# Operands of a latent attention made in the input projection, two or four heads per product, and kept in DRAM; of the split weights only the low parts stored

## The chip, the cores and the metric

The kernel runs on one core of one Trainium2 chip. Its time is the device time of one execution in microseconds (us). Three executions of the kernel before gave 2456.94, 2460.11 and 2461.5 us, so the median is 2460.11 us. A profile was taken of one further execution.

## What is computed

One decoder layer over 2048 positions of width 1024, in float32. The mixer joins four heads of a chunkwise mLSTM with eight heads of attention whose queries, keys and values come from small latents; a gated residual and a feed-forward layer of width 4096 follow.

```python
proj = rmsnorm(x, norm_pre_mix) @ w_in            # 1024 -> 1960 columns
qk_ml, v_ml, o_ml, gates = ...                    # mLSTM: conv + silu, chunkwise scan
c_q, c_kv, k_r = ...                              # latents: 256, 128 and 32 columns
q  = (rmsnorm(c_q, q_norm) @ w_uq).reshape(B, S, 8, 64 + 32)     # last 32: rotary
kv = (rmsnorm(c_kv, kv_norm) @ w_ukv).reshape(B, S, 8, 64 + 64)  # key part, value part
k  = concatenate([kv[..., :64], broadcast(apply_rope(k_r))])
h_mla = causal_softmax_attention(q, k, kv[..., 64:])
x = x + rmsnorm(concatenate([h_ml, h_mla]) @ w_out, norm_post_mix)
x = x + rmsnorm(relu(rmsnorm(x, norm_pre_mlp) @ w_up)**2 @ w_down, norm_post_mlp)
```

## The kernel before

**Number format.** TensorE multiplies in a reduced float32 format, so an operand is held as two tiles, a high part (a cast by ScalarE) and a low part (the value less the high part). A product is three matmuls, high by high, high by low and low by high. The helper `mm3` (L213 to L216) issues them, so most matmuls of the profile have the lines 214, 215 and 216, and the tile names tell them apart.

**Who sets the order.** Every piece of work is an operation of the planner `Plan` (L111): an engine, a cost, a key and what it waits for. At each step the planner takes the operation that can start first, and among those the one with the lowest key. It writes the instructions in that order, and each engine runs its own list in order. Most transfers are issued by SyncE (SP), in order too, so a store that waits for its data holds up the loads behind it.

**Input projection.** Four blocks of 512 positions. For each block, 16 units of weights of 128x1024 pass through. A unit (`unit`, L451) is eight `mm3`, 24 matmuls of 512 columns, into one of two PSUM banks (`mm`). VectorE or ScalarE empties the bank while the next unit fills the other. `values` (L890) makes the mLSTM values in the same way (tile `mv`). Weights come through `wsplit` (L400). In blocks 0 and 1 a unit is loaded raw, its high part cast by ScalarE (L416), its low part subtracted by VectorE or GpSimd (L421). In block 1 both parts are also stored in DRAM (`wparts`), and in blocks 2 and 3 both are loaded from there (`wload`, L383). `latents_in` (L561) makes the latents, and stores their two parts in DRAM (`cds`). Around these run the mLSTM chunks (`chunk`, L936; tiles `S`, `num`, `kv`, `ht`), four per block, whose state goes from chunk to chunk.

**Attention.** 320 steps: 8 heads, 4 blocks of queries and 4, 8, 12 or 16 blocks of 128 keys. A step is three matmuls of scores (tile `S`, L1515), two exponentials on ScalarE, one subtraction for the low part of the weights (`pl`, L1529, VectorE or GpSimd) and two or three matmuls with the values (`o`, L1542 to L1545). Before a head's steps its operands are made, on the same engines and between the steps of the head before:

- `prep_k` (L1419): three matmuls of 512 columns per head and block, with 64 columns of weights (tile `kk`), then a cast by ScalarE and a subtraction by VectorE.
- `prep_q` (L1382): six matmuls per head and block (tile `qq`). VectorE multiplies by a table of cosines and sines (`trig`), SP moves 32 rows to other partitions (`tr`), GpSimd adds, ScalarE casts and GpSimd subtracts (`Ql`, L1408).
- `vpair` (L1328): the values of four heads for two blocks of keys, six matmuls of 256 columns (tile `v`).
- `maxima` (L1443): for each head and block 4 to 16 matmuls (tile `m`, L1457) whose row maxima VectorE takes (L1462, L1464), which ScalarE then puts into a row of the queries. Their results pass through two banks (`m`).

The latents come back from DRAM through GpSimd's queue (`latents`, L1308; tile `c`).

**Between the two.** Memory changes hands in three switches (L1185 to L1223): `switch1` when the latents and weights are split, `switch2` after the last unit, `switch3` after the last chunk. Only then can scores, values and the odd heads' operands be placed.

## Time and profile before

| | |
|---|---|
| median of three executions | 2460.11 us |
| the profiled execution, its own time | 2458.44 us |
| its span in the trace | 2456.7 us |
| TensorE busy | 2396.5 us, 11059 matmuls |
| VectorE, ScalarE, GpSimd busy | 1773.2, 1330.1, 827.6 us |
| mean granted TensorE clock | 0.992 |
| moved by DMA | 404.36 MB |

The span runs from the first to the last recorded instruction. The input projection takes its first 453 us, the attention the next 530 or so, the output projection and the feed-forward layer the rest. "Busy" is the time in which at least one instruction of the engine is recorded. A matmul's recorded length is longer than its pitch, since the next begins before it ends: what a matmul costs is read from the distance between starts. A group's row gives line, engine, operation, tiles, shapes and count, then the busy time in us and the mean length of one in ns, then the engine's idle time ahead of the group and what ended it.

### The profile page before, as it was taken

Reading aid. Unit: us, or ns where it says so; the run is one execution under the profiler, and the core shown is the slowest. Engines: PE = TensorE matmul, PEld = TensorE weight load, DVE = VectorE, ACT = ScalarE, POOL = GpSimd, SP = SyncE. Lnnn points to the kernel's source line nnn. Section 1 sums busy time; section 2 is a strip of 40 time slices with the busy share of each in tenths; the row PEclk is TensorE's granted clock in tenths of the full one; section 3 lists DMA queues with packets and bytes.
Section 4 is the critical chain, followed back from the end, with each engine's and each line's share of the span. In section 5 each row is a group of like instructions: output and inputs, shape, how many; then the busy total and the mean of one; then the engine's idle time right before and its main releaser. Section 6 shows DMA issues by size and latency. Waiting matters only on the chain.

```text
span 2456.7 us, 33958 instructions
## 1 busy us (share of the span) xinstructions
PE 2396.5 (98%) x11059; PEld 1934.8 (79%) x11059; DVE 1773.2 (72%) x3171; ACT 1330.1 (54%) x2628; POOL 827.6 (34%) x728
## 2 busy tenths in 40 slices
PE   8999999899999999999999999999999999999996
PEld 6778788677777777678888888888888888888885
DVE  6876646578878887655876587776676687786888
ACT  5645222367777777544666656765665343433454
POOL 3432212468898888432100000000000232332334
PEclk9999999899999999999999999999999999999999
DMA  5688847500000000566776788756664535445369
GB/s 209 213 315 296 280 173 251 143 14 17 16 17 11 17 15 13 164 213 225 259 225 206 232 286 246 219 153 193 176 206 136 170 125 176 131 141 166 125 170 240
DMA packets 308266, 404.36 MB, mean 165 GB/s; under 512 B 32652, under 2 KB 209816, under 8 KB 307896
## 3 DMA queue, kind: packets, MB, share of 16 engines
q1 hardware_dynamic: 300760, 387.98, 49.3%
q0 software_dynamic: 7328, 14.21, 2.8%
q8 instruction: 87, 1.43, 0.2%
q14 instruction: 91, 0.75, 0.1%
HBM read 265.04 MB, written 134.96 MB: 163 GB/s over the span
## 4 chain that ended last, share of the span: by engine, by line
PE 80%; DVE 7%; DMA 5%; POOL 3%; issue 2%; ACT 2%; SPq 1%; DVEq 0%; POOLq 0%; ACTq 0%
PE mm L214 3%; PE mm L216 3%; PE mm L215 3%; PE S L214 2%; PE m L1457 2%; PE S L215 2%; PE S L216 2%; PE o L1542 2%; PE o L1545 2%; PE op L215 2%; PE op L214 2%; PE op L216 2%; POOL t L1556 2%; DMA hr<-hd 1%; PE mv L214 1%
## 5 line engine op out<-in xcount | busy, mean ns | idle before, releaser
L2436 POOL TENSOR_TENSOR y<-vd_0X,y 128x512 f32<-128x512 f32 x7 | 11.3, 1621 | 726.6 <-ACT vd_0X L2433 708.6
L1521 ACT ACTIVATE ph<-S 128x512 fp32r<-128x512 f32 (+1 forms) x320 | 170.3, 532 | 106.9 <-PE S L216 63.5
L1556 POOL TENSOR_TENSOR t<-t,ph 128x512 f32<-128x512 f32 (+1 forms) x192 | 211.0, 1099 | 24.2 <-ACT ph L1521 11.0
L2348 ACT CAST hh<-hr 128x512 fp32r<-128x512 f32 (+1 forms) x208 | 116.5, 567 | 170.7 <-DMA hr<-hd 46.3
L1529 DVE TENSOR_TENSOR pl<-S,ph 128x512 fp32r<-128x512 f32 (+3 forms) x272 | 157.3, 589 | 39.1 <-ACT S L1525 34.6
L214 PE MATMUL mm<-xh,wh 128*128 128x512 f32 x384 | 157.8, 411 | 11.5 <-ACT xh L358 6.7
L2353 DVE TENSOR_TENSOR hl<-hr,hh 128x512 fp32r<-128x512 f32 (+1 forms) x208 | 130.2, 635 | 38.6 <-ACT hh L2348 31.2
L1462 DVE TENSOR_REDUCE mp<-m 128x1 f32<-128x512 f32 x192 | 129.7, 684 | 33.0 <-PE m L1457 32.4
L216 PE MATMUL mm<-xh,wl 128*128 128x512 f32 x384 | 150.9, 393 | 0.2 <-DVE wl L421 0.2
L215 PE MATMUL mm<-xl,wh 128*128 128x512 f32 x384 | 151.1, 393 | 0.0
L1525 ACT ACTIVATE S<-S 128x512 f32<-128x512 f32 (+3 forms) x272 | 141.4, 520 | 0.0
L214 PE MATMUL S<-Qh,Kh 97*128 97x512 f32 (+1 forms) x320 | 123.1, 385 | 1.0 <-ACT p L1525 0.7
L1542 PE MATMUL o<-ph,V 128*128 128x512 f32 (+1 forms) x320 | 119.3, 373 | 0.0
L215 PE MATMUL S<-Ql,Kh 97*128 97x512 f32 (+1 forms) x320 | 119.0, 372 | 0.0
L1545 PE MATMUL o<-pl,V 128*65 128x512 f32 (+1 forms) x320 | 113.5, 364 | 5.5 <-DVE pl L1529 4.8
L216 PE MATMUL S<-Qh,Kl 97*128 97x512 f32 (+1 forms) x320 | 118.6, 371 | 0.0
L1457 PE MATMUL m<-Kh,Qh 96*128 96x512 f32 (+2 forms) x320 | 109.5, 382 | 1.1 <-DVE mp L1462 0.7
L2187 ACT ACTIVATE t<-t 128x512 f32<-128x512 f32 x96 | 60.6, 631 | 79.1 <-DVE t L2182 78.7
L214 PE MATMUL op<-wo,hh 128*128 128x512 f32 x256 | 101.2, 395 | 0.5 <-DVE x L1857 0.5
L215 PE MATMUL op<-wo,hh 128*128 128x512 f32 x256 | 100.0, 391 | 0.1
L216 PE MATMUL op<-wo,hl 128*128 128x512 f32 x256 | 100.0, 391 | 0.0
L214 PEld LDWEIGHTS mm<-xh,wh 128*128 128x128 f32 x384 | 72.7, 189 | 29.3 <-ACT xh L358 7.4
(6435 smaller groups left out, 7626.8 us busy)
## 6 DMA issues: line engine op xcount, KB each, us to landing
hr<-hd SPq DMA_DIRECT2D x100, 448.0 KB
hd<-t SPq DMA_DIRECT2D x128, 256.0 KB
hd<-ts SPq DMA_DIRECT2D x96, 256.0 KB
wh<-wparts SPq DMA_DIRECT2D x32, 512.0 KB
wl<-wparts SPq DMA_DIRECT2D x32, 512.0 KB
wr<-in_wu_dram SPq DMA_DIRECT2D x31, 512.0 KB
xt<-in_x_dram SPq DMA_DIRECT2D x28, 512.0 KB
xf<-xd SPq DMA_DIRECT2D x40, 256.0 KB
```

The costliest lines, as they stand in the source:

```text
L214: pe.matmul(o, ah, bh, start=start, stop=False)
L215: pe.matmul(o, ah, bl, start=False, stop=False)
L216: pe.matmul(o, al, bh, start=False, stop=stop)
L1457: pe.matmul(ps[:, :n], Qh[s][0:96, q0 : q0 + P], Kh[s][0:96, kb * TB : kb * TB + n], start=True, stop=True)
L1462: vec.tensor_reduce(mp["t"][:, j, kb : kb + 1], ps, axis=AX.X, op=ALU.max)
L1521: act.activation(t["h"][:, :w], t["S"][:, :w], AF.Exp)
L1525: act.activation(t["p"][:, :w], t["S"][:, :w], AF.Exp)
L1529: (pool if by_pool else vec).tensor_tensor(t["l"][:, :w], t["p"][:, :w], f32(t["h"][:, :w]), ALU.subtract)
L1542: pe.matmul(o0, v[:, 0:128], t["h"][:, :w], start=start, stop=stop)
L1545: pe.matmul(o1, v[:, 64:129], t["l"][:, :w], start=start, stop=stop)
L1556: pool.tensor_tensor(to, to, hv, ALU.add)
L2353: vec.tensor_tensor(t["l", m][:, :w], t["r", m][:, :w], f32(t["h", m][:, :w]), ALU.subtract)
```

## The change

The attention's operands are made during the input projection, block by block, right after the block's latents.

- Three weight units are added: 16 (keys and values), 17 (queries without their rotary part), 18 (rotary part). `operands` makes per block four key products of two heads each (`kp`, three matmuls), four value products of all eight heads for 128 positions each (`vp`, three), four query products of two heads (`qp`, six) and two rotary products of four heads (`rp`, six). They share the two banks of the units.
- A result is cast by ScalarE, copied by VectorE, and GpSimd subtracts the one from the other, in a staging tile (`sg`, four of them). SP then stores both parts in DRAM (`qkd`, `qrd`, `vd`). For rotary results VectorE multiplies three times and GpSimd adds first.
- In the attention `load_qk` and `load_v` load the finished operands; `prep_k`, `prep_q`, `prep_u`, `vpair`, `latents` and their tiles go. `maxima` gets the bank that they used as a third one.
- Weights: `wparts` holds the low parts alone. In blocks 1 to 3 (units 0 to 8) or 2 and 3 (the rest) a unit is loaded raw, ScalarE casts its high part each time, and the low part is loaded.
- To make room, the gates have one buffer in place of two and `hn` two in place of four. Some keys and leads of the planner are set anew, and the order of block 3 is written out.

```diff
-HN = 4
+HN = 2
...
-STB = (1,) * 16
+STB = (0,)*9+(1,)*10
+SG = 4
...
+LASTLINE = [16, "k0", "k1", 9, "k2", "k3", "v0", 10, "v1", "v2", "v3", 11, 17, "q0", "q1", 12, "q2", "q3", 18, "r0", "r1", 5, 6, 7, 8]
...
-    gate = [b1.tile([P, 4, TB], F32, tag=f"gate{i}", name=f"gate{i}") for i in range(2)]
+    gate = [b1.tile([P, 4, TB], F32, tag=f"gate{i}", name=f"gate{i}") for i in range(1)]
...
+        a = pl.op("SP", 500, load, [g], kA(b, at - WLEAD), kb=n / 2)
+        c = pl.op("Activation", n * 0.833 + 110, hi, [a], kA(b, at - SPLIT), take=("wh",), free=[("awr", g)])
+        gl = pl.op("X", 0, place_l, [g, *o_turn], kA(b, at - LLEAD), take=("wl",))
+        l = pl.op("SP", 500, load_l, [gl, *o_parts[u]], kA(b, at - LLEAD), kb=n / 2)
...
+        def product(u, passes, parts, nm, n, evac, key, head, o_in):
...
+            def mm(k):
+                if k == 0:
+                    q["p"] = psm.tile([P, TB], F32, tag="mm", name=f"{nm}{b}_{n}")
+                mm3(q["p"], *parts(k), k == 0, k == passes - 1)
...
+        def two_parts(nm, n, q, last, first, key, store, kb):
+            def hi():
+                act.copy(q["s"][:, 0], q["p"])
...
+            def raw():
+                vec.tensor_copy(f32(q["s"][:, 1]), q["p"])
...
+            def lo():
+                pool.tensor_tensor(q["s"][:, 1], f32(q["s"][:, 1]), f32(q["s"][:, 0]), ALU.subtract)
...
+            g = pl.op("X", 0, place, [last], key, take=("sg",))
+            h = pl.op("Activation", 570, hi, [g, last], key, free=[("mm", first)])
...
+            d = pl.op("DVE", 690, raw, [g, last], key, free=[("mm", first)])
+            d = pl.op("Pool", 1300, lo, [h, d], key)
...
+            return [pl.op("SP", 500, lambda i=i: store(i), [d], key, free=[("sg", h)], kb=kb) for i in range(2)]
...
+                x = pl.op("DVE", 690, a1_, [last, o_tb], key + PQ, take=("sg",), free=[("mm", first), ("cbc", o_tb)])
...
+                y = pl.op("DVE", 690, a2_, [last, o_tb], key + PQ, take=("cth",), free=[("mm", first), ("cbc", o_tb)])
+                z = pl.op("DVE", 690, a3_, [y], key + PQ, free=[("mm", first), ("cbc", o_tb)])
...
+    def load_qk(h, b, key):
+        s, bs, r = h % 2, slice(b * TB, (b + 1) * TB), slice(h % 4 * 16, h % 4 * 16 + 16)
...
         def load():
...
+            dma(f32(QK[s][0:64, :, bs]), qkd[h, :, :, bs])
+            for i in range(2):
+                dma(f32(QK[s][64 + 16 * i : 80 + 16 * i, 0:2, bs]), qrd[h // 4, 64 * i + r.start : 64 * i + r.stop, :, bs])
...
+                dma(f32(V[:, t + d, :, 0:128]), vd[t + d, :, 4 * g : 4 * g + 4])
...
-            pool.dma_start(both[b][:, i : i + n].rearrange("p i x t -> p (i x) t"), cds[b][2 * i : 2 * i + 2 * n].rearrange("x p t -> p x t"))
...
-        a = pl.op("PE", 6 * 228, mm, [o_u[h][0], o_cl[0, b], o_cl[1, b], o_s3 if s else o_s2] + war, key, take=(qring("q", h),), free=[("uq", o_u[h][1])])
...
-        a = pl.op("PE", 3 * 228, mm, [o_uk, o_cl[2, b], o_s3 if s else o_s2] + war, key, take=(qring("k", h),))
...
+        def ring(i):
+            return "q" if (h, qb) in EARLY or i % 3 == 2 else "m"
```

How the change moves instructions is shown at two places. The first is VectorE's list in block 2, from the emptying of unit 9's bank (`mm2_9`). Before:

```order
L932 TENSOR_TENSOR gate0_117<-mm2_9_2838,rsbc2_2092 128x512
L875 SCALAR_TENSOR_TENSOR kT0_115<-cth2_3_2919,cy2_3_2877 128x512
L929 TENSOR_SCALAR gate0_117<-gate0_117,col_61 128x512
L932 TENSOR_TENSOR gate0_117<-mm2_10_2890,rsbc2_2092 128x512
L929 TENSOR_SCALAR gate0_117<-gate0_117,col_61 128x512
```

And in the change, where `kp2_2`, `kp2_3` and `vp2_0` are products, `ks` and `vs` their staging tiles, and the rows of `sm22_2` and `kw2_3` belong to the mLSTM:

```order
L1131 TENSOR_TENSOR gate0_116<-mm2_9_3471,rsbc2_2446 128x512
L1224 TENSOR_TENSOR sm22_2_3535<-sm22_2_3535 128x4
L1225 TENSOR_SCALAR sm22_2_3535<-sm22_2_3535 128x4
L1226 SCALAR_TENSOR_TENSOR sm22_2_3535<-sm22_2_3535 128x4
L1197 SCALAR_TENSOR_TENSOR kw2_3_3578<-kt2_3_3563,tm2_3121 128x256
L1128 TENSOR_SCALAR gate0_116<-gate0_116,col_61 128x512
L730 COPY ks2_2_3568<-kp2_2_3556 128x512
L730 COPY ks3_2_3582<-kp2_3_3573 128x512
L781 COPY vs0_2_3597<-vp2_0_3589 128x8x64
L382 SCALAR_TENSOR_TENSOR xl3_0_3620<-xr3_0_3522,col_61,xh3_0_3609 128x512
L382 SCALAR_TENSOR_TENSOR xl3_1_3626<-xr3_0_3522,col_61,xh3_1_3618 128x512
L1131 TENSOR_TENSOR gate0_116<-mm2_10_3593,rsbc2_2446 128x512
```

Between the emptyings of two units' banks three further banks are now to be emptied, and the first of them stands behind the gate's second step (L1128), which waits for ScalarE. The second place is TensorE's list from the last chunk's products on (`num3_3`: numerators of chunk 3 of block 3; `ht3_3`: its turned result). Before, queries and keys of head 0 (`qq0_0`, `kk0_1`) follow:

```order
L988 MATMUL num3_3_4286<-C1_111,qs3_3_4201 128x258
L1005 MATMUL kv3_3_0_4299<-vext_112,kw3_3_4278 128x258
L214 MATMUL qq0_0_4306<-c_0_3995,uqh0_4023 128x512
L215 MATMUL qq0_0_4306<-c_0_3995,uqh0_4023 128x512
L216 MATMUL qq0_0_4306<-c_0_3995,uql0_4028 128x512
...
L1005 MATMUL kv3_3_1_4322<-vext_112,kw3_3_4278 128x258
L1044 MATMUL ht3_3_4339<-cst_60,hn3_3_4335 128x128 x4
L214 MATMUL kk0_1_4344<-c_1_4250,ukh_3993 64x512
...
L214 MATMUL qq0_1_4353<-c_1_4250,uqh0_4023 128x512
```

In the change the maxima of head 0 follow (`m0_1_0_0` is head 0, block 1 of queries; `QK0` holds the loaded operands):

```order
L1187 MATMUL num3_3_5011<-C1_110,qs3_3_4935 128x258
L1204 MATMUL kv3_3_1_5031<-vext_111,kw3_3_4993 128x258
L1527 MATMUL m0_0_0_0_5057<-QK0_4983 128x128
L1527 MATMUL m0_0_1_0_5059<-QK0_4983 128x256
L1527 MATMUL m0_0_2_0_5061<-QK0_4983 128x384
L1243 MATMUL ht3_3_5064<-cst_60,hn3_3_5053 128x128 x4
L1527 MATMUL m0_0_3_0_5070<-QK0_4983 128x512
L1527 MATMUL m0_1_0_0_5075<-QK0_4983 128x512
L1527 MATMUL m0_1_1_0_5080<-QK0_4983 128x512
L1527 MATMUL m0_1_0_1_5085<-QK0_4983 128x128
```

Queries, keys and values have left the opening of the attention; what stands there until the first scores is the maxima, each of which VectorE has to reduce.

More of the change, by code (lines that the diff above doesn't have):

```diff
@@ L594, in sums_ @@
                     pe.matmul(t["p"][:, i * 4 + c : i * 4 + c + 1], q["s"][:, c * P : (c + 1) * P], ones[:, 0:1], start=True, stop=True)
[L596 removed]
+            take = () if i else ("sg", "sg")
+            if i == 0 and b:
+                t["o"] = list(o_staged[b - 1])
             if b == 0:
@@ L890, in values @@
     def values(b):
-        ws = [W[b, 5 + i] for i in range(4)]
+        ws = [WT[b, 5 + i] for i in range(4)]
         def one(c):
@@ L1141, in half @@
             prev.append(o)
-            o_rope.append(pl.op("SP", 1000, store, [o], key, free=[("cth", h)], kb=256))
+            o = pl.op("SP", 1000, store, [o], key, free=[("cth", h)], kb=256)
+            o_rope.extend((o, pl.op("SP", 3000, spread, [o], key, kb=1024)))
         prev = []
@@ L1257, in trunk @@
         o_const[s] = pl.op("Pool" if s == "v" else "SP", 490 if s == "v" else 1500, fill, [o_s3 if s else o_s2], key=-99 if s == 0 else -50, kb=0 if s == "v" else 24)
-    def load_w(nm, src):
-        raw = a2.tile([P, 512], F32, tag="craw", name=f"{nm}r", bufs=2)
-        dma(raw, src)
-        wts[nm] = [raw, *wts[nm]]
-    def weights(nm, src, key, after):
-        a = pl.op("SP", 500, lambda: load_w(nm, src), [after], key=key, take=("craw",), kb=256)
-        b = pl.op("Activation", 615, lambda: act.copy(wts[nm][1], wts[nm][0]), [a], key)
-        return pl.op("DVE", 680, lambda: vec.tensor_tensor(wts[nm][2], wts[nm][0], f32(wts[nm][1]), ALU.subtract), [b], key, free=[("craw", a)])
-    o_uk = weights("uk", ukw, -90, o_s1)
-    o_uv = weights("uv", uvw, -60, o_s2)
     blocks, first, start_of = [], {}, {}
```

446 lines of the change are left out of this document (231 added, 215 removed).

## The prediction

> **What bounds the kernel now.** I read the page first, then busy time by stretches, then the waits and the chain where the stretches showed gaps, and last the groups for durations.
>
> ```profile
> span 2456.7 us, 33958 instructions
> PE 2396.5 (98%) x11059; PEld 1934.8 (79%) x11059; DVE 1773.2 (72%) x3171; ACT 1330.1 (54%) x2628; POOL 827.6 (34%) x728
> ```
>
> TensorE (PE) is recorded busy 98% of the span, so 60 us are all the idle time there is. Recorded busy time proves little by itself where matmuls overlap, so I checked the pitch. These are the first and the last of 37 consecutive starts in the input projection:
>
> ```profile
> 179.62 0.39 PE L214 MATMUL mm<-xh,wh 128*128 128x512 f32 x1
> ...
> 187.78 0.39 PE L214 MATMUL mm<-xh,wh 128*128 128x512 f32 x1
> ```
>
> 36 pitches take 8.16 us, 0.227 us each; the recorded 0.39 us contains the pipeline's delay. The stretches show where PE has gaps. The columns are the stretch and its length, then busy time and count of PE, weight loads, VectorE (DVE), ScalarE (ACT) and GpSimd (POOL), then granted clock, DMA share and GB/s:
>
> ```profile
> 120.00:180.00 60.00, 57.43 (x275) 46.34 (x274) 44.13 (x89) 25.22 (x37) 21.25 (x16) 1.00 0.88 323
> 180.00:240.00 60.00, 59.65 (x285) 49.57 (x284) 40.00 (x85) 31.42 (x80) 18.28 (x20) 1.00 0.81 285
> 240.00:300.00 60.00, 59.59 (x286) 48.02 (x285) 40.46 (x90) 19.02 (x38) 14.27 (x18) 1.00 0.88 304
> 360.00:420.00 60.00, 59.82 (x278) 48.15 (x278) 37.29 (x82) 14.75 (x30) 13.74 (x17) 1.00 0.74 256
> 454.00:464.00 10.00, 6.71 (x40) 5.27 (x39) 6.70 (x19) 2.88 (x11) 6.24 (x9) 1.00 0.81 192
> 464.00:484.00 20.00, 15.62 (x63) 10.39 (x61) 11.06 (x29) 7.90 (x18) 9.52 (x15) 0.74 0.89 229
> 484.00:504.00 20.00, 18.22 (x83) 14.64 (x84) 14.53 (x32) 9.26 (x20) 9.52 (x9) 0.83 0.07 18
> 504.00:531.00 27.00, 25.36 (x114) 18.79 (x113) 21.63 (x46) 15.29 (x32) 14.10 (x13) 0.87 0.05 11
> 700.00:900.00 200.00, 199.57 (x1046) 155.41 (x1045) 163.65 (x363) 150.62 (x315) 170.38 (x148) 1.00 0.07 15
> ```
>
> Two things stand there. The input projection and the running attention are bound by PE, at full clock, with the other engines at most 85% busy. So a matmul taken out of the attention shortens it, and one put into the projection lengthens that. The opening of the attention, 454 to 531 us, is not. Busy time times clock gives 6.7 + 11.6 + 15.1 + 22.1 = 55.5 us of work in 77 us, so 21.5 us are lost there to idleness and to the lower clock.
>
> **Matmuls removed and added.** The groups of the products that go, each for the first of the three lines of `mm3`:
>
> ```profile
> L214 PE MATMUL qq<-c,uqh 128*128 128x512 f32 x64 | 27.3, 426 | 2.1 <-DMA c<-cd 2.0
> L214 PE MATMUL kk<-c,ukh 128*64 128x512 f32 x32 | 13.2, 413 | 0.4 <-DVE tq L1395 0.4
> L214 PE MATMUL v<-uvh,c 128*128 128x256 f32 x32 | 10.0, 313 | 0.8 <-DVE V L1344 0.6 <-DVE Kl L1434 0.2
> ```
>
> Times three that is 192 matmuls of 512 columns for queries, 96 for keys, and 96 of 256 columns for values, which I count as 48 of 512. Together 336. Added per block are 4x3 for keys, 4x3 for values, 4x6 for queries and 2x6 for rotary parts, 60, in four blocks 240. The key product used 64 columns of weights and has the same recorded length as the query product with 128, so two heads in one cost what one did; that halves the keys, and with the swapped rotary columns dropped the queries go from 192 to 144. Net 96 fewer, at 0.227 us: **-21.8 us**. I take it whole, because both ends of the move lie in PE-bound stretches; only some 14 us of the removal (36 of `qq` and `kk` for head 0 and 48 narrow ones of `v`) lie in the opening and are treated with it.
>
> **Waits in the input projection.** The 56 new products share two banks with the units. Before, a bank had a unit of 24 matmuls, 5.4 us, to be emptied in; a key or value product lasts 0.68 us. The waits of today and the prices:
>
> ```profile
> L214 PE MATMUL mm<-xh,wh 128*128 128x512 f32 x384 | 157.8, 411 | 11.5 <-ACT xh L358 6.7 <-DVE raw L852 4.7
> L932 DVE TENSOR_TENSOR gate<-mm,rsbc 128x512 f32<-128x512 f32 x16 | 11.0, 688 | 11.1 <-PE mm L216 11.0
> L933 ACT ACTIVATE gate<-gate 128x512 f32<-128x512 f32 x16 | 10.1, 629 | 20.3 <-DVE gate L932 20.1
> L929 DVE TENSOR_SCALAR gate<-gate,col 128x512 f32<-128x512 f32 x16 | 8.5, 530 | 4.4 <-ACT gate L933 4.1
> L1619 DVE COPY ou<-o 65x512 f32<-65x512 f32 x32 | 21.8, 682 | 10.0 <-PE o L1545 6.7 <-issue 1.2 <-POOL Ql L1408 1.1
> L1408 POOL TENSOR_TENSOR Ql<-tq,Qh 96x512 fp32r<-96x512 f32 x32 | 41.2, 1289 | 11.6 <-ACT Qh L1405 11.0 <-PE o L1568 0.5
> ```
>
> And the way from a product through a copy to the next product, in the chain:
>
> ```profile
> 469.33 0.44 PE qq L216
> 469.80 0.70 DVE tq L1395
> 470.54 0.61 PE kk L214
> ```
>
> After a recorded end DVE starts 0.03 us later, and PE 0.04 us after DVE's end. With the pipeline's delay of 0.16 (0.39 less 0.227), a bank is free 0.93 us after PE has passed its last matmul, if DVE is at hand. Follow block 2 in the order shown. PE passes unit 9 at 0, then `kp2_2` to 0.68; `kp2_3` wants unit 9's bank, 0.93: a wait of 0.25 less the mLSTM work between. `vp2_0` wants the bank of `kp2_2`, whose copy stands behind the gate's second step: 0.19 + 0.69 + 0.04 + 0.63 + 0.04 + 0.53 + 0.68 + 0.04 = 2.84, against PE's 1.6 to 2.0: a wait of about 1. Then `mm2_10` waits 0.1. The group of three values waits some 0.5 by the same count. The queries, 1.36 us each, hide a prompt copy; the second rotary product leaves three multiplications, 2.0 us, before the next block's second bank: about 1. With the pair at the start, 3 us per block, 12 in four. If DVE or ACT has another instruction of 0.7 us ahead in half of these places, 16 to 20. mLSTM work between the products hides part. I take **+13 us**, with ends of 4 and 30.
>
> The other engines have room: DVE gains 48 copies and 24 multiplications, 50 us, ACT 56 casts and 44 more casts of weights, POOL 64 instructions of 1.3 us, over a stage whose rows above show them below three quarters busy. DMA is nearer its end. By the sizes of its tiles a block of the change moves about 35 MB (raw weights 9.7, low parts 9.7, operands 7.3, x 4.2, mLSTM and tables 4), where blocks 2 and 3 moved 26. The raw weights are read in every block now. In the rows above share and rate give 323/0.88 = 367, 285/0.81 = 352, 304/0.88 = 345, 256/0.74 = 346: about 350 GB/s at a full share. 35 MB then take 100 us, and a block lasts some 125. So DMA bounds no block on average, and I add nothing, with +5 as an end for bursts.
>
> **The opening of the attention.** Now PE waits there for the last chunk and for latents that come through GpSimd's queue:
>
> ```profile
> PE ht L1044 <- DVE hn L1037: 3.3, 1, 3.3
> ```
>
> ```profile
> 457.69 0.72 POOL c L1312
> 458.41 8.32 DMA c<-cd
> 466.86 0.76 PE qq L214
> ```
>
> In the change the loads of head 0 are on SP's list ahead of the last chunks' stores, and the chain latent, product, multiplication, move, addition, cast is gone. The wait for `ht` stays, and with three narrow maxima (0.35 us) in place of the query product (1.4) as its cover it grows by 1. After it come maxima with nothing between them, and they go at VectorE's pace:
>
> ```profile
> L1462 DVE TENSOR_REDUCE mp<-m 128x1 f32<-128x512 f32 x192 | 129.7, 684 | 33.0 <-PE m L1457 32.4
> ```
>
> Seven more until the first scores, up to 0.68 us each against PE's 0.23: 3 us lost. With the 4.3 of `ht` and some 2 for the way from the last maximum over ScalarE to the first scores that is 9, and for half clock behind such gaps and waits among the later reductions I add 6 to 7. The later opening is eased: DVE loses 16 instructions of 0.68 us (4 `tq`, 4 `Kl`, 8 `V`) and 4 additions, over 11 us out of the 47 that the rows give it from 464 to 531. So the loss is 15 to 16 us in place of 21.5: **-6 us**, ends -14 and +6. The Trainium skill, "TensorE: Matmul & The Clock Gate", Part 1, says that the array falls to half clock after an idle window of about 3.4 us and needs as long a busy one to come back. The 0.74 in the row fits that; by it, as an estimate, the longer `ht` wait alone would cost 1.7 us more than I count, and the sum would be -13.1 in place of -14.8.
>
> **The rest.** From the end of the opening, near 531, the attention stays bound by PE. Its DVE, ACT and POOL work falls with PE's, so their shares stay near today's 82, 75 and 85%. The loads of operands, 30 MB over some 450 us, find DMA at a share of 0.07. Later stages are untouched.
>
> **Sum.** -21.8 + 13 - 6 = -14.8. The profiled execution took 2458.4 us (span 2456.7 and 1.7 around it), which gives 2443.6. The median of the runs lies 1.7 above it, so I forecast **2445 us**.
>
> **Rivals.**
> - *The opening gains more, or the waits stay hidden.* For it: PE had 11 us of plain idle time in 454 to 531, much of it behind the latents, and the mLSTM's matmuls lie between the products in blocks 0 to 2. Against: reductions bind the maxima. With -12 and +5: 2431.
> - *The waits eat the gain.* VectorE's list is in order, and a copy also stands behind `xl` of the next block, which needs a load. At half a microsecond per new product, 28 us and -6, nothing is left: 2460.
> - *Staging holds the banks: slower.* A copy needs one of four staging tiles, free when the product four earlier is stored. Copy 0.7, one to three subtractions in line 1.3 to 3.9, and the store. The only landing time of the trace is of a loaded moment:
>
> ```profile
> c<-cd POOLq DMA_DIRECT2D x1, 512.0 KB, 5.8
> ```
>
>   That makes 7.8 to 10.4 us, where PE reaches the same tile again after 8 to 9 us in the tightest places. If stores land 3 us later than this, three products per block wait 3 us each, 36 us in all on top of the 13: 2481. It decides from about 4 us of extra waiting per block, which cancels the 14.8. Today's stores already hold ScalarE's casts for 5.7 us, which speaks for it:
>
> ```profile
> L416 ACT CAST wh<-wr 128x1024 fp32r<-128x1024 f32 x31 | 32.4, 1044 | 28.6 <-PE mm L215 18.6 <-DMA wparts<-wl 5.7 <-PE mv L216 2.0
> ```
>
>   Against it, a tile waits for four products, most of which have a unit of 5.4 us between them. The Trainium skill, "DMA: Bandwidth & Descriptors", Anatomy of one DMA, fits a transfer by some 2.0 us and its bytes over 436 GB/s: 3.2 us for these 512 KB, where the trace has 5.8. By the page the chain would be 5.2 to 7.8 us as an estimate, PE would never wait for it, and I would give this case 0.12.
> - *The change does not do what it says.* Storing low parts alone leaves the bytes as they are; that is in the sum already.
>
> **Chances.** The forecast, 2432 to 2454: 0.50. Opening or hiding better, below: 0.18. Waits eat the gain, 2455 to 2465: 0.14. Staging and other slower cases: 0.18. A measurement of this kernel tells some 0.2%, 5 us, from no change. Faster by more: 0.68; within: 0.14; slower: 0.18. The range leaves out about a tenth at either end: the better case's own lower half below 2427, the staging case's upper half above 2470.
>
> **What would show it.** Right: PE's matmuls fall by 144; the products `kp`, `vp`, `qp`, `rp` have a pitch of 0.227; idle time before `mm` and the products grows by 10 to 15 us, released by DVE and ACT; the stretch from the last unit to the last maxima of head 0 falls from 77 to about 60 us. Staging: waits of DVE `ks` and `vs` on DMA. DMA: weights `wl` or `wh` release PE. Wrong: a total above 2455, or an opening that takes as long as now.

## The result and the profile after the change

| | before | change |
|---|---|---|
| median of 5 runs each | 2460.51 us (2456.94 to 2461.5) | 2472.6 us (2466.99 to 2473.14) |
| profiled execution: time, span | 2458.4, 2456.7 us | 2470.98, 2469.2 us |

The ratio is 1.0046, with a 95% interval of 1.0032 to 1.0061: the change is slower by half a per cent. The prediction was 0.6% faster. (Measured once more beside the last experiments, the change stood at 1.0058, 1.0043 to 1.0074.) The new page begins:

```profile
span 2469.2 us, 34097 instructions
## 1 busy us (share of the span) xinstructions
PE 2391.8 (97%) x10915; PEld 1920.1 (78%) x10915; DVE 1769.7 (72%) x3160; ACT 1359.8 (55%) x2638; POOL 811.1 (33%) x705
```

PE has 144 matmuls fewer, as counted, and almost the busy time of before: the recorded busy time of a matmul stretches where it waits or runs at half clock, so the busy share hides the loss. To find it, cut both traces at the same events. From the groups by tile: the last product of the projection's values (`mv`), the reduction that closes the maxima of a block of queries (`mx`), and the first transpose behind the attention (`xtr`). The two times in a row are the first and the last start. Before:

```profile
L216 PE MATMUL mv<-wh,xl x128: 388/389/402, 76.2 to 453.2; 128*128 128x512 f32 x128
L1908 PE MATMUL xtr<-cst,x x64: 270/273/332, 1072.1 to 1136.7; 128*128 128x128 f32 x64
530.90 0.17 DVE L1483 TENSOR_REDUCE mx<-mp 128x4 fp32r<-128x16 f32 x1
```

And in the change:

```profile
L222 PE MATMUL mv<-wh,xl x128: 388/390/629, 62.4 to 538.8; 128*128 128x512 f32 x128
L1971 PE MATMUL xtr<-cst,x x64: 270/273/330, 1085.0 to 1151.6; 128*128 128x128 f32 x64
591.17 0.16 DVE L1553 TENSOR_REDUCE mx<-mp 128x4 fp32r<-128x16 f32 x1
```

With the last `mx`, at 985.6 us before and at 995.9 us in the change, this gives:

| stretch | before | change | difference | the prediction's terms |
|---|---|---|---|---|
| input projection, to the last `mv` | 453.2 | 538.8 | +85.6 | +54.4 matmuls, +13 waits = +67.4 |
| opening, to the last maxima of head 0 | 77.7 | 52.4 | -25.3 | -13.6 matmuls, -6 = -19.6 |
| heads 1 to 7 | 454.7 | 404.7 | -50.0 | -62.7 matmuls |
| to the first `xtr` | 86.5 | 89.1 | +2.6 | 0 |
| the rest | 1384.6 | 1384.2 | -0.4 | 0 |
| sum | 2456.7 | 2469.2 | +12.5 | -14.8 |

(Matmul terms: 240 added and 336 removed, of which 60 in the opening, at 0.227 us.) Of the 27.3 us between forecast and result the projection has 18.2, the heads 1 to 7 have 12.7, the tail 2.2, and the opening gave 5.7 more than expected. A second profile of the changed kernel, told of below, differs from this one by 2 us in the projection and by 3 in the opening; smaller differences between single profiles are not read here.

**The projection.** 85.6 us less 54.4 us of new matmuls leaves 31 us. The view of PE's waits in this stretch (sum, number, longest), for the change and then for before:

```profile
...
PE kp L220 <- DVE raw L1051: 3.6, 1, 3.6
PE mm L220 <- ACT ks L727: 2.9, 4, 1.5
PE mm L221 <- DVE xl L382: 2.7, 4, 0.7
PE mv L220 <- DVE raw L1051: 2.4, 1, 2.4
PE kv L1204 <- DVE kw L1197: 2.2, 2, 1.6
PE vp L220 <- DVE gate L1131: 1.4, 1, 1.4
...
PE vp L220 <- ACT vs L778: 1.0, 3, 0.4
...
```

```profile
...
PE mm L214 <- DVE raw L852: 4.7, 4, 1.7
PE tp L764 <- DVE rrc L491: 1.5, 1, 1.5
...
```

`raw`, a bank of the mLSTM's convolution, was waited for before as well. New among the releasers are the copies and casts of operands (`ks`, `vs`) and the gates whose banks the products take. The idle times in this view leave out the pipeline's delay, so I also went over all pitches of consecutive matmuls up to the last `mv` and took from each what its kind needs undisturbed (0.2265 us for 512 columns). The excess is 66.2 us, before 37.1. Waits of units and products for an operand or gate bank are 15.7 of it, in 32 places (none before). Pitches of big matmuls without any wait hold 23.7, before 16.7. Waits for weights and inputs hold 4.8, before 1.2. The rest, 22.0 and 19.2, lies at the mLSTM's small matmuls, its waits and the banks of its convolution (`raw`). The first unit starts 1.35 us later, too.

Half clock is part of the 7.0 us by which the pitches without a wait grew. It can be seen behind the longest of these waits, in PE's timeline of the change:

```profile
457.19 0.39 PE L221 MATMUL kp<-cl,wh 128*128 128x512 f32 x1
457.42 0.40 PE L222 MATMUL kp<-ch,wl 128*128 128x512 f32 x1
461.41 0.79 PE L220 MATMUL kp<-ch,wh 128*128 128x512 f32 x1 [3.59 <-DVE raw L1051]
462.00 0.63 PE L221 MATMUL kp<-cl,wh 128*128 128x512 f32 x1
...
464.13 0.63 PE L220 MATMUL mm<-xh,wh 128*128 128x512 f32 x1
```

Ahead of the wait the pitch is 0.23 us; behind it five pitches from 462.00 to 464.13 take 0.426 each, so every such matmul costs nearly its own length again. How much of the projection ran so is told by the granted clock (the figure after the engines' counts), below 1.00 in three stretches of the change:

```profile
60.00:90.00 30.00, 27.08 (x121) 21.94 (x122) 27.96 (x47) 15.58 (x34) 11.37 (x15) 0.94 0.67 214
450.00:480.00 30.00, 24.83 (x99) 18.50 (x97) 23.36 (x31) 13.31 (x27) 13.00 (x12) 0.94 0.66 196
480.00:510.00 30.00, 29.21 (x118) 23.08 (x119) 14.16 (x23) 12.95 (x19) 12.35 (x11) 0.94 0.87 280
```

Before, it was 1.00 from 60 to 453 us. Six hundredths of 30 us are 1.8 us, so the clock cost the projection 5 us at most; the 17 pitches between big matmuls that ran at half clock hold 3.7. About as much again is the first pitch behind a wait, which is some 0.11 us longer at full clock too: 39 such pitches, six before.

**Two readers take turns.** This is the piece of the change's timeline in which block 0 makes its third and fourth key products (the second column is the duration):

```profile
110.06 0.40 PE L222 MATMUL kp<-ch,wl 128*128 128x512 f32 x1
110.50 0.69 DVE L730 COPY ks<-kp 128x512 f32<-128x512 f32 x1
...
111.11 0.40 PE L222 MATMUL kp<-ch,wl 128*128 128x512 f32 x1
...
111.22 0.58 ACT L727 CAST ks<-kp 128x512 fp32r<-128x512 f32 x1 [1.74 <-DVE ks L730]
...
111.55 0.69 DVE L730 COPY ks<-kp 128x512 f32<-128x512 f32 x1 [0.28 <-PE kp L222]
111.83 1.28 ACT L1132 ACT_TABLE_LOAD   x1
111.86 0.50 PE L220 MATMUL vp<-wh,ch 128*128 128x512 f32 x1 [0.35 <-ACT ks L727]
...
113.66 0.57 ACT L727 CAST ks<-kp 128x512 fp32r<-128x512 f32 x1
```

VectorE copies the bank and ScalarE casts it, each straight from the bank, and the cast begins 0.03 us after the copy has ended though ScalarE sat idle for 1.74 us. A bank is thus held for 0.69 + 0.03 + 0.58 = 1.30 us, not for 0.69. For the last product it is worse: between copy (111.55) and cast (113.66) ScalarE loads a table and computes a gate. So both the turns and the place in an engine's list can hold a bank; the experiments with casts take them apart.

**Heads 1 to 7.** From one head's last maxima to the next the change takes 56.3 to 56.8 us, but head 4 takes 65.0. The heads' share of the view of waits has one entry that fits, and the timelines of SP, then of VectorE, ScalarE and PE, show its cause:

```profile
PE o L1612 <- DVE ot L1685: 6.6, 1, 6.6
```

```profile
780.76 8.47 SPq L1500 DMA_DIRECT2D V<-vd  x6
...
790.71 1.14 SPq L1500 DMA_DIRECT2D V<-vd  x2
...
795.08 4.84 SPq L1500 DMA_DIRECT2D V<-vd  x4
800.64 2.30 SPq L1695 DMA_DIRECT2D hT<-ot  x1
```

```profile
805.12 0.69 DVE L1689 COPY ou<-o 65x512 f32<-65x512 f32 x1 [4.23 <-DMA sumd<-ou]
807.40 0.58 ACT L1682 COPY ot<-o 64x512 f32<-64x512 f32 x1 [7.19 <-DMA hT<-ot]
808.84 0.76 PE L1612 MATMUL o<-ph,V 128*128 128x512 f32 x1 [6.57 <-DVE ot L1685]
```

The values of heads 4 to 7 take the place of those of heads 0 to 3, so their 16 loads of 256 KB, the first four issued at 774.75 us, can start only as the last products of head 3 release them. The output rows `ot` and `ou` have one buffer each; their stores stand behind these loads, and the next rows can't be moved out of PE's banks until they have landed. The stretches around it (length, busy time and count of PE, loads, DVE, ACT and POOL, clock, DMA share, GB/s):

```profile
780.00:802.00 22.00, 21.04 (x112) 15.60 (x111) 16.32 (x37) 14.56 (x32) 15.43 (x13) 1.00 1.15 224
802.00:808.00 6.00, 0.27 (x2) 0.10 (x1) 0.69 (x1) 0.58 (x1) 0.07 (x1) 0.83 0.67 166
808.00:812.00 4.00, 3.16 (x9) 2.31 (x10) 2.54 (x5) 2.25 (x6) 2.75 (x3) 0.50 0.17 35
```

DMA is full for 22 us at 224 GB/s, PE then stands still for 6.6 us, and after that runs at half clock.

### The profile page after: what moved, and what is told of

Read it like the earlier page. It is cut to its first block, busy times and chain, and to the rows that moved or that the text cites. A ratio compares the mean times of both kernels' runs of the same rounds, so it can differ in the third digit from the quotient of the medians.

```text
span 2469.2 us, 34097 instructions
## 1 busy us (share of the span) xinstructions
PE 2391.8 (97%) x10915; PEld 1920.1 (78%) x10915; DVE 1769.7 (72%) x3160; ACT 1359.8 (55%) x2638; POOL 811.1 (33%) x705
## 3 DMA queue, kind: packets, MB, share of 16 engines
q1 hardware_dynamic: 341448, 446.98, 58.4%
## 4 chain that ended last, share of the span: by engine, by line
PE 78%; DVE 7%; DMA 6%; issue 3%; POOL 2%; ACT 2%; SPq 1%; DVEq 0%; POOLq 0%; ACTq 0%
PE S L220 2%; PE o L1612 2%; PE mm L220 2%; PE o L1615 2%; PE S L221 2%; PE S L222 2%; PE mm L222 2%; PE mm L221 2%; PE m L1527 2%; PE op L220 1%; PE op L222 1%; PE op L221 1%; DMA hr<-hd 1%; PE mv L220 1%; PE mv L221 1%
## 5 line engine op out<-in xcount | busy, mean ns | idle before, releaser
L1591 ACT ACTIVATE ph<-S 128x512 fp32r<-128x512 f32 (+1 forms) x320 | 170.2, 532 | 97.2 <-PE S L222 28.9
L1599 DVE TENSOR_TENSOR pl<-S,ph 128x512 fp32r<-128x512 f32 (+3 forms) x272 | 157.0, 590 | 30.9 <-ACT S L1595 28.9
L2416 DVE TENSOR_TENSOR hl<-hr,hh 128x512 fp32r<-128x512 f32 (+1 forms) x208 | 130.2, 635 | 36.6 <-ACT hh L2411 28.9
L220 PE MATMUL S<-QK 97*128 97x512 f32 (+1 forms) x320 | 123.7, 386 | 5.9 <-DVE pl L1599 4.7
L221 PE MATMUL S<-QK 97*128 97x512 f32 (+1 forms) x320 | 118.6, 371 | 0.0
L1527 PE MATMUL m<-QK 96*128 96x512 f32 (+3 forms) x320 | 114.9, 405 | 3.4 <-DVE mp L1532 1.8
L222 PE MATMUL S<-QK 97*128 97x512 f32 (+1 forms) x320 | 118.1, 369 | 0.0
```

The costliest lines, as they stand in the source:

```text
L220: pe.matmul(o, ah, bh, start=start, stop=False)
L221: pe.matmul(o, ah, bl, start=False, stop=False)
L222: pe.matmul(o, al, bh, start=False, stop=stop)
L1527: pe.matmul(ps[:, :n], Qh[s][0:96, q0 : q0 + P], Kh[s][0:96, kb * TB : kb * TB + n], start=True, stop=True)
L1591: act.activation(t["h"][:, :w], t["S"][:, :w], AF.Exp)
L1599: (pool if by_pool else vec).tensor_tensor(t["l"][:, :w], t["p"][:, :w], f32(t["h"][:, :w]), ALU.subtract)
```

## The experiments

The ratios are each to runs of the kernel before on the same chip, with 95% intervals; the change's own is 1.0046. One per mille is 2.5 us. "Excess" is the sum over pitches in the projection explained above (change 66.2 us, before 37.1), "bank waits" are its part of 15.7.

**No emptying of the banks.** In `two_parts`, `vevac` and `revac` the moves go; a blank tile, in the place of one of the four staging tiles, is stored.

```diff
...
-            h = pl.op("Activation", 570, hi, [g, last], key, free=[("mm", first)])
...
-            d = pl.op("DVE", 690, raw, [g, last], key, free=[("mm", first)])
-            d = pl.op("Pool", 1300, lo, [h, d], key)
...
-            return [pl.op("SP", 500, lambda i=i: store(i), [d], key, free=[("sg", h)], kb=kb) for i in range(2)]
+            pl.op("X", 0, lambda: None, [last], key, free=[("mm", first)])
+            return [pl.op("SP", 500, lambda i=i: store(i), [last, blank_op[0]], key, kb=kb) for i in range(2)]
```

> Leaves out the emptying of the operand banks: the 240 new matmuls run, but no copy, cast, subtraction or rotary multiplication follows; one blank tile is stored in the place of every operand, with the same bytes, and the attention loads and multiplies those zeros. All times on the scale on which the kernel before takes 2460.5 us and the change 2472.6. Theory evacuation (banks held by copy and cast, and the clock's fall behind these waits): the projection's excess over pure matmul time falls from 66 us to 45 or less, 2448 to 2453 us. Rival (loads and DMA make the excess): it stays above 58 and the time above 2463.

Measured 0.996 (0.9945 to 0.9975), 22 us below the change, on that scale 2450.7. The excess is 40.1 us, three more than before the change:

```profile
L222 PE MATMUL mv<-wh,xl x128: 388/389/628, 62.9 to 511.7; 128*128 128x512 f32 x128
```

The last `mv` starts at 511.7, which is 58.5 us after that of before, with 54.4 us of new matmuls. So matmuls, weights, and all the bytes that are loaded and stored cost next to nothing beyond PE's own time. (The profiled execution took 2455.68 us, 9 more than the median of the seven, and its opening 6 us more than the change's, so its total gained less than its projection.) What the forecast missed in the projection is the emptying, whole: 26 us of excess against a forecast of 13. This run doesn't tell the hold of the banks from the other work that emptying gives VectorE, ScalarE and GpSimd.

**Cast from the copy.** The cast reads SBUF, so that the bank has one reader.

```diff
-                act.copy(q["s"][:, 0], q["p"])
+                act.copy(q["s"][:, 0], f32(q["s"][:, 1]))
...
-            h = pl.op("Activation", 570, hi, [g, last], key, free=[("mm", first)])
...
             d = pl.op("DVE", 690, raw, [g, last], key, free=[("mm", first)])
+            h = pl.op("Activation", 570, hi, [g, d], key)
```

(Values in the same way.)

> The cast to the high part of keys, values and queries reads the copy in SBUF instead of the PSUM bank, so a bank is free after VectorE's copy (0.69 us) and no longer after copy and cast in turn (1.30 us). Theory bank time (the 15.7 us of waits of products and units for operand copies come from two readers taking turns): these waits fall to 6 to 9 us, the clock loses 1 to 2 us less behind them, and the time is about 2463 us. Rival, queue order (the copies are late because VectorE and ScalarE have other work ahead of them): the waits stay above 13 us and the time within 3 us of 2472.6.

Measured 1.0047 (1.0032 to 1.0063): no gain, as the rival had it, but not for its reason. Bank waits still sum to 15.6 us, in 14 places in place of 32, and half of that is one wait. The change has it in a smaller form: ScalarE's cast of the last value waits there for a store, until 128.75 us, and PE waits 0.84 us behind it (at 130.11). VectorE's, SP's and PE's timelines there:

```profile
128.52 0.69 DVE L781 COPY vs<-vp 128x512 f32<-128x512 f32 x1 [2.95 <-DMA qkd<-ks]
```

```profile
113.95 4.53 SPq L1335 DMA_DIRECT2D trep<-trigd  x6
...
119.25 4.61 SPq L757 DMA_DIRECT2D qkd<-ks  x4
```

```profile
129.36 0.77 PE L220 MATMUL mm<-xh,wh 128*128 128x512 f32 x1 [7.77 <-DVE vs L781]
```

The copy of a value waits for a staging tile, which is free when the store of a key has landed, and that store stands in SP's queue behind the six stores that spread the rotary tables in block 0. Here four of the eight key stores of this block stand behind them, in the change two (issued at 120.05 us). The remaining 13 places hold 7.7 us, which is what bank time foretold. The gain at the other places was lost at this one.

**One reader.** VectorE's copy is left out and GpSimd subtracts the cast from itself.

```diff
-                pool.tensor_tensor(q["s"][:, 1], f32(q["s"][:, 1]), f32(q["s"][:, 0]), ALU.subtract)
+                pool.tensor_tensor(q["s"][:, 1], f32(q["s"][:, 0]), f32(q["s"][:, 0]), ALU.subtract)
...
-            d = pl.op("DVE", 690, raw, [g, last], key, free=[("mm", first)])
-            d = pl.op("Pool", 1300, lo, [h, d], key)
+            d = pl.op("Pool", 1300, lo, [h], key)
```

(Values in the same way.)

> Leaves out VectorE's copy of keys, values and queries: ScalarE's cast alone reads the bank, GpSimd subtracts the cast from itself (zeros as low parts), with the same staging, stores and rotary work. Same scale; without any emptying the time was 2450. Theory bank time: a bank is held 0.6 instead of 1.3 us, bank waits fall to 5 to 8 us, 2458 to 2464. Rival staging and lists (ScalarE, GpSimd and the stores set the pace): waits above 12 us, 2468 to 2473.

Measured 1.0039 (1.0026 to 1.0052). Again a single wait takes much of the gain, at the same place; it is ScalarE's cast that lacks the tile here:

```profile
PE mm L220 <- ACT vs L777: 5.7, 1, 5.7
```

Bank waits are 14.2 us with it, 8.3 without. (The profiled execution, 2465.05 us, is one of the two fastest of five, the others took 2470 to 2471; its projection ends 5.1 us before the change's.) This run and the one before agree: halving the hold halves the waits, and staging then caps the gain. The earlier run took ScalarE's list out of the bank's way and this one VectorE's, with the same outcome, which points to the two turns rather than to the list of one engine.

**The tables' stores aside.** The six stores go through GpSimd's queue.

```diff
-                        dma(to, trigd[r0 : r0 + 16, cs].rearrange("(o j) t -> o j t", o=1).broadcast_to((n, 16, 512)))
+                        pool.dma_start(to, trigd[r0 : r0 + 16, cs].rearrange("(o j) t -> o j t", o=1).broadcast_to((n, 16, 512)))
...
-            o_rope.extend((o, pl.op("SP", 3000, spread, [o], key, kb=1024)))
+            o_rope.extend((o, pl.op("Pool", 6000, spread, [o], key, kb=1024)))
```

> The change with one edit: the six stores of the rotary tables go through GpSimd's queue, casts and output buffers as in the change. Scale as before (kernel before 2460.5, change 2472.6; early casts alone 2472, two buffers alone 2468.5, all three 2456.5). Theory staging behind the banks: with late casts PE already waits at the banks while the stores land, so the edit alone brings 0 to 3 us, 2469 to 2473. Rival (the stores in SP's queue delay weights and other loads by themselves): 2461 to 2465, and the bank waits of block 0 fall too.

Measured 1.0079 (1.0064 to 1.0093): 5 to 8 us slower than the two measurements of the change, which neither theory had. Bank waits are 21.7 us, and four of them in block 0, between 111 and 128 us, hold 7.5. GpSimd's timeline shows why:

```profile
110.30 3.73 POOL L1335 DMA_DIRECT2D trep<-trigd  x6
...
115.07 2.52 POOL L733 TENSOR_TENSOR ks<-ks 128x512 fp32r<-128x512 f32 x2
```

The issues take GpSimd for 3.7 us, the subtractions of keys stand behind them, and so the stores of keys start no earlier; VectorE's copy of a value (126.66) then waits 3.2 us for its staging tile. So the edit doesn't free the tiles sooner by itself. That explains the projection, which ends 4.4 us later than the change's; the opening and the heads 1 to 7 took 4.0 and 4.5 us more in this profile (of the slowest execution of the run), and why is open.

> Early casts and the tables through GpSimd's queue, one output buffer. Same scale. Theory: the two belong together, the shorter hold shows only once the staging wait of 8 us is gone; 2459 to 2463, with head 4 still at 65 us. Rival (the gain of all three edits came from the two buffers and chance in the order): 2468 to 2472.

With early casts as well: 1.0034 (1.0021 to 1.0048), 2468.9 us on the scale of the expectations, in the rival's range; the interval overlaps the change's. The wait of 7.8 us for staging has become one of 4.3, and head 4 still takes 63.4 us.

**Two output buffers.**

```diff
...
-... ("ot", 1, o_s3), ("ou", 1, o_s3), ...
+... ("ot", 2, o_s3), ("ou", 2, o_s3), ...
...
-            t["u"] = xrow("ou") if end else ar2.tile([P, TB], F32, tag="ou", name=f"ou{h}_{qb}", bufs=1)
+            t["u"] = xrow("ou") if end else ar2.tile([P, TB], F32, tag="ou", name=f"ou{h}_{qb}", bufs=2)
```

(`ot` in the same way.)

> The output rows of a head (ot, ou) have two buffers each instead of one. Theory burst (the 6.6 us wait of PE for ot in head 4 comes from the store of one buffer standing behind 4 MB of value loads): this wait goes, with the clock's fall behind it 7 to 9 us, about 2464.5 us, and the period of that head becomes 57 us like the others. Rival (the values themselves come too late): PE waits for V or the scores instead, the head stays at 65 us and the time at 2472.

Measured 1.003 (1.0019 to 1.004). The 6.6 us wait is gone, heads 1 to 7 take 396.2 us instead of 404.7, and head 4 takes 60.7; the six others take 335.5 together instead of 339.7, so the single buffer cost them something too. The total gained 4 us of these 8.5; the opening took 3.5 us longer in this profile, which the change's own second profile shows as scatter.

**No second load of values.**

```diff
-                    load_v(h // 4, t, W[start_of[h, qb]] - VLEAD - LDK)
+                    if h:
+                        o_v[1, t] = o_v[0, t]
+                    else:
+                        load_v(0, t, W[start_of[h, qb]] - VLEAD - LDK)
```

> Leaves out the second load of values: heads 4 to 7 use the values of heads 0 to 3 that lie in SBUF. Same scale. Theory burst: PE's 6.6 us wait for ot goes, head 4 takes 57 us like the others, 2463 to 2465. Rival (one output buffer is too few whatever the DMA does): a wait of 3 us or more for ot stays in head 4, and the time is within 3 us of 2472.6.

Measured 1.0032 (1.002 to 1.0043). Head 4 takes 56.3 us, heads 1 to 7 take 396.0, and the wait for `ot` falls from 7.5 us in the whole attention to 2.8. It is the burst: with one buffer and without the loads the wait of 6.6 us does not exist.

**Two banks for the maxima.**

```diff
-            return "q" if (h, qb) in EARLY or i % 3 == 2 else "m"
+            return "q" if (h, qb) in EARLY else "m"
```

> The maxima use two banks, as before the change, the third stays empty. Theory (the third bank eases every run of maxima in which VectorE is the slower one): the opening of the attention, 52.4 us from the last unit to the last maxima of head 0, grows by 3 to 6 us, and PE's idle time before maxima in the other heads by 2 to 6; 2478 to 2484 us in all. Rival (VectorE's pace binds the maxima whatever the number of banks): within 3 us of 2472.6.

Measured 1.0082 (1.0067 to 1.0097), 6 to 9 us slower than the two measurements of the change. The opening takes 55.6 us, no more than in the change's second profile, so nothing is seen of the theory there. Heads 1 to 7 take 406.8 instead of 404.7, and this sum hides two things: head 4 takes 61.1 us instead of 65.0, and the six others 345.7 together instead of 339.7, each of them longer (57.4 to 58.3, where the change's two profiles have 56.3 to 56.8). So the third bank is worth about 1 us in each such head; PE's idle time before maxima, 1.2 us against 1.3 in these heads, is not what makes it, so the theory's mechanism is not shown, and the cause is open.

**Pairs between units.**

```diff
-MIXED = [16, "k0", "k1", 9, "k2", "k3", "v0", 10, "v1", "v2", "v3", 11, 17, "q0", "q1", 12, "q2", "q3", 18, "r0", "r1"]
+MIXED = [16, "k0", "k1", 9, "k2", "k3", 10, "v0", "v1", 11, "v2", "v3", 12, 17, "q0", "q1", "q2", "q3", 18, "r0", "r1"]
```

(`LASTLINE` in the same way.)

> Keys and values stand in pairs between units (two keys, unit 9, two keys, 10, two values, 11, two values, 12) instead of 2, 3 and 3; all queries follow. Same scale. Theory bank time: a third product in a row is the one that waits, so bank waits fall from 15.7 to 8 to 11 us, and the time to 2464 to 2469. Rival: the waits come from VectorE's and ScalarE's lists and move to other places; within 3 us of 2472.6.

Measured 1.0155 (1.0137 to 1.0174), 27 us slower than the change. The excess is 92.3 us, and new entries head the waits:

```profile
PE mm L220 <- ACT wh L452: 11.8, 3, 8.1
PE mm L220 <- DVE rt L837: 5.1, 2, 2.9
```

Unit 12 waits for its weights (some 1.9 us in each of blocks 0 to 2; the 8.1 is the start of the kernel): there are four buffers, unit 16's is held to the last value, and with 9, 10 and 11 in between unit 12 is the fifth. The next block's first unit waits for rotary multiplications, now that six products of queries and rotary parts follow each other. Bank waits are 17.0 us. The order by itself costs more than the whole change lost.

**Copies first.** `PQ = 5.0` becomes `PQ = -20.0`.

> The key of the operand copies (PQ) is -20 instead of 5, so the planner puts them ahead of other work of VectorE and ScalarE that is ready at the same time. Same scale. Theory queue order: bank waits fall from 15.7 to 10 or less and the time to 2462 to 2467. Rival bank time (a bank waits for copy and cast however early they stand): waits within 3 us, 2469 to 2476, or more where the work passed over is late.

Measured 1.0074 (1.006 to 1.0088). Bank waits are 19.3 us in 31 places. Putting copies ahead doesn't shorten them, so VectorE's and ScalarE's lists are not the cause by way of their priorities. The mLSTM work that was passed over makes PE wait instead: `kv` for `kw` grows from 2.2 to 3.9 us.

**Both parts stored.** `wparts` holds both parts again, `wload` loads them into `wh` and `wl`, no cast.

```diff
-        c = pl.op("Activation", n * 0.833 + 110, hi, [a], kA(b, at - SPLIT), take=("wh",), free=[("awr", g)])
+        c = pl.op("SP", 500, load, [g, *o_parts[u]], kA(b, at - LLEAD), kb=n / 2)
```

> Both parts of the weights are stored and loaded again, as before the change: 45 casts of 1.05 us leave ScalarE in the input projection, 19 stores of 512 KB come in. Theory queue order (ScalarE's list holds casts of weights that wait for PE, 44 us of waiting at that line, and operand casts stand behind them): bank waits fall by 4 to 8 us, the time is 2465 to 2469. Rival bank time: ScalarE's casts of operands come at the same moments, waits within 2 us, time 2471 to 2476, the upper end if the added stores (10 MB, 28 us of DMA at 350 GB/s) delay loads in the first two blocks.

Measured 1.0173 (1.0154 to 1.0193), 31 us slower than the change, beyond all that was expected. The projection ends at 567.7 us with an excess of 96.6: bank waits 22.8, pitches without any wait 36.7. The granted clock is 0.70 to 0.85 in four stretches of 30 us (60 to 120 and 180 to 240), where the change has 0.94 in one of them and 1.00 in the others: from 204.2 to 228.1 us it stood at 0.50 throughout, with waits of 1.0 to 2.9 us in that time. The pitches of big matmuls at half clock hold some 20 us there, 3.7 in the change, so more than half of the 28.9 us by which this projection is longer is clock. The planner gave all engines another order with this edit, so the run gives no sign that ScalarE's casts of weights hold the change back, and no more; where its waits come from stays open.

**Combinations.** Early casts, two output buffers and pairs:

> Three edits together: casts read the SBUF copy, two output buffers, pairs between units. Same scale. If they add: bank waits below 8 us, no 6.6 us wait in head 4, 2456 to 2461, about the kernel before. Rival staging (a copy now waits for a staging tile whose store has not landed, 8 us at one place in the run with early casts): such a wait stays, 2463 to 2468.

Measured 1.0111 (1.0096 to 1.0126), 11 us better than the pairs alone, and 16 us slower than the change: the pairs' waits stay (the longest: weights 3.2 us, rotary 3.6 and 3.1), and no edit on copies reaches them.

Early casts, two output buffers and the tables' stores aside, in the change's own order:

> Early casts and two output buffers, and the six stores that spread the rotary tables go through GpSimd's queue, since in the run with early casts they stood in SP's queue ahead of key stores and VectorE's copy of a value waited for a staging tile (PE 7.9 us). Scale as before (kernel before 2460.5, change 2472.6). Theory: without that staging wait the shorter hold shows, bank waits at 6 to 9 us; with the 4 us of the two buffers 2458 to 2463. Rival (the waits move on to another place, order and not hold decides): 2466 to 2470.

Measured 0.9984 (0.9976 to 0.9993): 2454.94 us where the kernel before took 2457.97. Three more kernels ran in the same rounds as each other, to tell what of that belongs to which edit. Early casts and two buffers without the table edit:

> Early casts and two output buffers, the tables' stores in SP's queue as in the change. Scale as before (kernel before 2460.5, change 2472; all three edits 2456.6). If the tables' stores decide: the staging wait of 8 us in block 0 stays and the time is 2464 to 2468. If the two output buffers bring most once the casts are early (heads 1 to 7 in 395 us): 2457 to 2462, and the table edit is worth 3 us or less.

The change itself:

> The changed kernel itself, on the same chip and in the same rounds as the two combinations, so that they can be compared with it directly. 1.0046 of the kernel before, as first measured, within 0.0015; if it differs by more, gains of 3 us between earlier runs are not to be read.

And the three edits once more:

> The three edits again, in the same rounds. If the gain is of the edits: 0.997 to 0.9995 of the kernel before, and the last values' product starts at 530 to 533 us. If the 4 us by which its projection was shorter than in the run without the two buffers, with the same order of instructions there, were chance: 534 to 537, and 0.9995 to 1.002.

| in the same rounds | median | ratio, interval | last `mv` | heads 1 to 7 |
|---|---|---|---|---|
| change | 2470.16 us | 1.0058 (1.0043 to 1.0074) | 540.9 | 405.5 |
| early casts, two buffers | 2459.78 | 1.001 (1.000 to 1.002) | 538.7 | 395.0 |
| and tables aside | 2456.07 | 0.9996 (0.9988 to 1.0005) | 531.4 | 394.9 |

Two edits bring 10.4 us, which is the heads' 10.5, and the table edit 3.7 more, in the projection, where the staging wait falls from 6.8 us to 3.7. The row of the last `mv` is the same as in the first run of the three edits, to 0.1 us, so the 4 us were no chance of that run:

```profile
L222 PE MATMUL mv<-wh,xl x128: 388/389/418, 62.5 to 531.4; 128*128 128x512 f32 x128
```

In two measurements this version is 0.16% and 0.04% below the kernel before, the first outside its interval and the second not: it takes back what the change lost and is at best a few us ahead. What is left in its projection (waits of the first run, again sum, number, longest):

```profile
...
PE vp L220 <- DVE vs L781: 3.6, 1, 3.6
PE kp L220 <- DVE raw L1051: 3.5, 1, 3.5
...
PE mm L220 <- DVE ks L730: 2.2, 1, 2.2
...
PE vp L220 <- DVE gate L1131: 2.1, 1, 2.1
```

## Why the prediction was wrong, step by step

**Matmuls: right.** 144 instructions fewer and 0.227 us for each. Without emptying, the projection grew by 58.5 us with 54.4 of matmuls in it.

**Waits in the input projection: the step that failed first.** "I take +13 us, with ends of 4 and 30"; it was 31, or 26 by the run without emptying. Three things were missing from it.
- The hold of a bank. "A bank is free 0.93 us after PE has passed its last matmul" counted VectorE's copy alone. The trace has copy and cast in turn, 1.30 us, so 1.5 us with the delays. The code showed the two readers: `hi` and `raw` both read `q["p"]`. The Trainium skill says why they take turns, "PSUM — Partial Sum Buffer", in the section on bank collisions: two engines may not access one bank's quadrant at the same time, two reads included, so they have to be put in turn. The rows at 110.50 and 111.22 agree with it, with 0.03 us between the two.
- The clock. I charged half clock in the opening but not in the projection, because the clock of before was 1.00 there. Waits bring it down: it fell to half in three stretches, each behind waits, which cost 5 us at most, and the first pitch behind each wait is longer as well. Together the pitches without any wait grew by 7.0 us, a little under half of the bank waits. The Trainium skill, "TensorE: Matmul & The Clock Gate", Part 1, has the idle window of about 3.4 us; behind the wait of 3.59 us the pitch was 0.426, which agrees. The two other stretches don't: their half clock set in behind a wait of 2.39 us (at 61.59) and behind two of 1.35 and 0.25 us (at 480.44 and 481.65), so here less idle time was enough.
- Work beside the products. Waits for inputs and weights grew by 3.6 us. The rotary multiplications stand ahead of `xl` of the next block in VectorE's list; I had named this and priced it at 1 us per block, as a bank. `xl` itself was late too: the one that begins at 280.68 us took 1.89 us, where the median is 0.75, while a rotary addition of GpSimd ran beside it (280.72 to 282.01). Whether the one is the reason of the other was not tried, but without these 1.1 us PE's wait of 0.67 us behind it would not have been.

The bank waits themselves, 15.7 us, came near the 13. That is partly luck, since the hold was longer than in my sum; I take it that the mLSTM work between the products hid more than I allowed, which no run shows. The parts add up: 15.7 us at the banks, 7.0 of slower pitches, 3.6 for inputs and weights, 2.8 more at the mLSTM and 1.35 at the start are 30.5 of the 31.

**The opening: right in kind, too small.** 77.7 us became 52.4 in one profile and 55.4 in the other, where I expected about 60. Where the rest comes from was not tried apart; the run with two banks opened in 55.6.

**Heads 1 to 7: the second step that failed.** "The loads of operands, 30 MB over some 450 us, find DMA at a share of 0.07" is an average. The values come in two bursts, and the second one is squeezed by the buffers that it reuses into 25 us. I looked for a wait of PE for the values; it was the store of another tile, in the same queue and with a single buffer, that was late. The heads gave back 12.7 us, 8.4 of them in head 4. Two output buffers bring back 8.5 of them, 4.2 in the six heads beside it, so the single buffer cost a little in every head and not in the burst alone.

**The rivals.** "The waits eat the gain" put 28 us of waits into the projection, which was close to what happened; together with the burst the time went past its 2460. "Staging holds the banks" named a mechanism that exists but not at that price: in the change it is behind 0.84 us of PE's waits, at 130.11 us, after a cast that stood for 2.97 us. With early casts it is 4 to 8 us at one place. I had it decide "from about 4 us of extra waiting per block"; it came to one wait in block 0, from stores of tables in the queue and not from slow stores as such.

What stays open: where the waits come from that lowered the clock in the run with both parts stored; why two output buffers bring 4 us alone and 10 with early casts, which alone brought none; and the 3 us by which the opening differs between two profiles of one kernel. The last two may be one question. In the profiles the heads 1 to 7 gain nearly the same from two buffers, 8.5 us alone and 10.5 with early casts. What differs is the opening, 55.9 us against 52.7: in all six profiles with early casts it took 52.3 to 53.0 us, in the eleven of the other versions 51.3 to 58.4. Why early casts should settle it was not tried.

## What to carry to other kernels

When work is moved into a stage that PE fills, price not its matmuls but the time for which each result holds its bank: count every reader of the bank in turn, and add what follows each wait, a longer first pitch and now and then a stretch at half clock. Give a bank one reader and let the other read the copy; but look for what holds the same place next, since here this edit halved the other bank waits and was worth nothing in the total while a staging tile was late. Where loads replace work, look for the moment at which the buffers they reuse come free: an average share says nothing about a burst, and whatever has a single buffer and a store in the same queue waits with it.

## What was not expected of the hardware

The 16 loads of values go in pieces of 512 bytes per partition and head (128 columns, at a pitch of 129 in SBUF). With the DMA engines full (share 1.15 from 780 to 802 us) they and the loads beside them moved 224 GB/s, where the projection before the change moved about 350 at a full share. Whether the short pieces are the reason was not tried. The store that stood behind them took from 800.6 us, its issue, to about 807.4, when ScalarE's next copy could start, for 128 KB.
